# Splitting the last 384 columns of one 2 MB load into transfers of 119 and 9 rows, in a mixture of softmaxes on one core

## The chip, the core and the metric

The kernel runs on one core of a Trainium2 chip, the seven other cores idle. The metric is the device time of one execution in microseconds (us). Before the change it is 787.27 us, the median of three runs between 787.08 and 787.27 us.

## What is computed

There are 32 units (the batch). A unit has 128 rows, four heads and 4096 columns. In each row every head's 4096 logits go through a softmax; the four softmaxes are added, weighted by a softmax over the four numbers of `prior` in that row.

```python
def reference(logits, prior):            # (32, 128, 4, 4096), (32, 128, 4)
    prior_probs = softmax(prior)         # over the four heads
    softmax = np.exp(logits - logits.max(axis=-1, keepdims=True))
    softmax = softmax / softmax.sum(axis=-1, keepdims=True)
    return np.sum(prior_probs[..., None] * softmax, axis=2)   # (32, 128, 4096)
```

The input is 268.4 MB and the output 67.1 MB, all float32, and every byte moves once between HBM (the chip's main memory) and SBUF (the core's on-chip memory).

## The kernel before

The 128 rows of a unit are the 128 partitions of SBUF. The buffer `ring` has 12 slots; a slot holds one head of one unit, 128 x 4096 float32 (2 MB), so the ring holds three units. `place` (L106 of the kernel before) says which slot a head gets; `load` (L115, issuing at L120) brings heads that lie in neighbouring slots in one transfer of up to 8 MB.

A head goes through these steps: `peak` (VectorE, L128) takes the negated maximum of a row; `exp` (ScalarE, L133) exponentiates in place and sums; `recip` (VectorE, L139) inverts the sum. Heads 0 to 2 are then scaled and added up by TensorE: `diagonal` (GpSimd, L142) writes the scale on a diagonal matrix and `weigh` (L151) multiplies it with the exponentials into the accumulator `acc`. Head 3 is scaled by GpSimd (`scale`, L162) or directly by VectorE (L168). `evac` (ScalarE, L187) copies the accumulator out and `add_scaled` (GpSimd, L190) adds head 3 to it, in head 3's own slot; from that slot the unit is stored (L125).

The order of all this is written by hand: words such as `M3` (peak of head 3) or `L03+2` (load heads 0 to 2 of the unit after next) in the strings FIRST, STEADY and ORDER. All loads are issued by the sync engine's queue (SP). Stores of units 2 to 21 are issued by ScalarE's queue, the others by SP. At the start SP issues the four heads of unit 0 one by one (FIRST), then unit 1 in one transfer of 8 MB, then heads 0 to 2 of unit 2 (6 MB) and its head 3 (2 MB); ScalarE's queue issues the small load of `prior` beside the first. Later loads wait until their slots are free.

The transfers run on 16 DMA engines, which all queues share. A transfer of 128 rows is cut into 16 shares of 8 rows; each share reports its landing by itself, and whoever waits for the transfer waits for all 16 reports. The framework counts these reports on eight semaphores that the transfers take in turn; a transfer that takes one up again waits for the one that held it.

Of the kernel before, what the change touches and what calls it, by code (L numbers as in the profile page):

```python
# [63 lines left out]
    "R3@31 C3@31 T23@31 X112@31 T34@31 X212@31 A01@31 S23@31 A12@31 S34@31 S01@31 S12@31 "  # L64
]

BYPASS = {
    (27, 3), (28, 2), (28, 3), (29, 3), (30, 3), (31, 2), (31, 3),
}
# [3 lines left out]
def kernel(  # L73
# [6 lines left out]
    nc = tc.nc  # L80
    U, P, H, V = logits.shape
# [24 lines left out]
    def place(u, h):  # L106
        return (4 * u + h + (u == U - 1 and h == H - 1)) % SLOTS

    def slot(u, h, a=0, b=4):
        return ring[:, place(u, h), a * C : b * C]  # L110
# [2 lines left out]
        return slot(u, 3, a, b)  # L113

    def load(u, h=0, to=H):  # L115
        while h < to:
            s, n = place(u, h), 1
            while h + n < to and place(u, h + n) == s + n:
                n += 1
            nc.sync.dma_start(out=ring[:, s : s + n], in_=logits[u, :, h : h + n, :])  # L120
            h += n
# [26 lines left out]
    def weigh(u, h, a=0, b=4):  # L148
        e = slot(u, h)
        for k in range(a * C // W, b * C // W):  # L150
            nc.tensor.matmul(  # L151
                acc[:, k * W : (k + 1) * W], lhsT=diag[:, u % 2, h],
                rhs=e[:, k * W : (k + 1) * W],
                start=h == 0, stop=h == H - 2 or (u, k * W // C) in BYPASS and h == H - 3,
            )
# [33 lines left out]
    def add_scaled(u, a, b):  # L189
        nc.gpsimd.tensor_add(home(u, a, b), slot(u, 1, a, b), slot(u, 3, a, b))  # L190

    step = {
        "L": load, "S": store, "M": peak, "E": exp, "R": recip, "G": diagonal, "X": weigh,
        "C": weight, "Z": scale, "A": add_last, "B": add_head, "T": add_both, "V": evac,
        "P": add_scaled, "W": add_second,
# [11 lines left out]
    with tc.manual_schedule():  # L207
# [6 lines left out]
            out=ident, in_=ident, pattern=[[-1, P]], compare_op=ALU.is_equal, fill=0.0,  # L214
# [48 lines left out]
```

## Time and profile before

| | |
|---|---|
| median of three runs | 787.27 us |
| the profiled execution | 786.99 us |
| its span, first to last instruction | 785.2 us (so 1.75 us lie around it) |
| mean granted TensorE clock | 0.965 |
| moved | 335.90 MB, 428 GB/s over the span |
| busy: TensorE, VectorE, ScalarE, GpSimd | 679.0, 644.2, 548.0, 296.9 us |

The profile is one execution, taken by the hardware profiler. Beside the instructions the trace has each DMA packet (in this kernel, mostly one row of a transfer) with its start, length and size, though not the number of its DMA engine, and the moments at which the 16 shares of each transfer report. Where a time of a share or a packet is told below, it is read from these; times count from the first instruction.

### The profile page before, as it was taken

The numbers are of one execution on the slowest core, as the hardware profiler recorded it, in microseconds if no ns is written. First come the engines' busy times: TensorE is split into PE (matmuls) and PEld (weight loads), VectorE is DVE, ScalarE is ACT, GpSimd is POOL, SyncE is SP. The second block draws the span as 40 slices with busy tenths as digits, with TensorE's granted clock in tenths as the row PEclk, the third lists the DMA queues.
The fourth block names the chain that finished last, engine by engine and source line by source line (L and its number), as shares of the span: only waits on it lengthen the run. The fifth ranks groups of instructions, "written<-read, shape, count | busy, mean of one in ns | idle before, by whom it ended". The sixth has DMA issues, their size and how long they took to land.

```text
span 785.2 us, 4590 instructions
## 1 busy us (share of the span) xinstructions
PE 679.0 (86%) x1508; PEld 291.8 (37%) x1508; DVE 644.2 (82%) x326; ACT 548.0 (70%) x327; POOL 296.9 (38%) x244
## 2 busy tenths in 40 slices
PE   0959998888998989989889898998978998899996
PEld 0424444333443333434334333343333433334342
DVE  6489877897778977779877798777888877979895
ACT  2566876867668666687676776766857668779883
POOL 0053333433134332334323343323430544277892
PEclk9979999999999999989999999999989999999999
DMA  9999999999999999999999999999999999999998
GB/s 377 451 417 426 452 416 423 431 446 430 437 417 432 440 437 437 427 420 437 444 422 446 410 435 451 425 431 420 432 440 442 425 418 431 444 419 429 429 427 340
DMA packets 15336, 335.90 MB, mean 428 GB/s; under 512 B 1713, under 2 KB 1713, under 8 KB 2257
## 3 DMA queue, kind: packets, MB, share of 16 engines
q1 hardware_dynamic: 12384, 293.61, 87.1%
q10 hardware_dynamic: 2928, 42.01, 12.5%
q8 instruction: 12, 0.20, 0.1%
q14 instruction: 12, 0.09, 0.0%
HBM read 268.50 MB, written 67.11 MB: 427 GB/s over the span
## 4 chain that ended last, share of the span: by engine, by line
DMA 58%; DVE 12%; PE 10%; POOL 10%; issue 6%; ACT 3%; SPq 0%; POOLq 0%; ACTq 0%
DMA ring<-in_logits_dram 58%; DVE nmax L128 12%; PE acc L151 10%; POOL ring L190 7%; ACT ring L187 2%; ACT ring L133 1%; POOL ring L184 1%; POOL ring L162 1%; POOL diag L142 1%; DVE ring L168 0%; SPq L120 0%; DVE rden L139 0%; SPq L125 0%; POOLq L190 0%; POOLq L142 0%
## 5 line engine op out<-in xcount | busy, mean ns | idle before, releaser
L151 PE MATMUL acc<-ring,diag 128*128 128x512 f32 x1508 | 679.0, 611 | 99.3 <-ACT ring L187 63.7
L128 DVE TENSOR_REDUCE nmax<-ring 128x1 f32<-128x4096 f32 x128 | 563.1, 4409 | 115.9 <-DMA ring<-in_logits_dram 115.9
L133 ACT ACTIVATE ring<-ring,nmax 128x4096 f32<-128x4096 f32 x128 | 474.6, 3708 | 203.7 <-DVE nmax L128 203.3
L151 PEld LDWEIGHTS acc<-ring,diag 128*128 128x128 f32 x1508 | 291.8, 196 | 485.6 <-issue 356.3
L190 POOL TENSOR_TENSOR ring<-ring 128x1024 f32<-128x1024 f32 x69 | 162.3, 2371 | 19.6 <-ACT ring L187 12.9
L142 POOL TENSOR_SCALAR diag<-ident,rden,pp 128x128 f32<-128x128 f32 x96 | 42.9, 448 | 237.5 <-DVE rden L139 237.5
L158 POOL TENSOR_TENSOR wght<-rden,pp 128x1 f32<-128x1 f32 x33 | 6.2, 189 | 209.5 <-DVE rden L139 209.5
L187 ACT ACTIVATE ring<-acc 128x1024 f32<-128x1024 f32 x69 | 67.4, 1010 | 16.2 <-PE acc L151 12.0
L162 POOL TENSOR_SCALAR ring<-ring,rden,pp 128x2048 f32<-128x2048 f32 (+3 forms) x35 | 75.1, 2146 | 9.4 <-DVE rden L139 9.4
L168 DVE SCALAR_TENSOR_TENSOR ring<-ring,wght,acc 128x1024 f32<-128x1024 f32 x59 | 73.2, 1270 | 3.0 <-PE acc L151 1.3
L139 DVE RECIPROCAL rden<-dsum 128x1 f32<-128x1 f32 x128 | 19.3, 153 | 10.1 <-ACT ring L133 10.1
L133 ACT ACTIVATION_READ_ACCUMULATOR ring<-ring,nmax 128x1 f32 x128 | 24.2, 189 | 0.0
L184 POOL TENSOR_TENSOR ring<-ring 128x1024 f32<-128x1024 f32 x5 | 11.9, 2373 | 0.1
L218 DVE TENSOR_REDUCE pmax<-pr 32x128 f32<-32x512 f32 x1 | 0.7, 674 | 5.2 <-DMA pr<-in_prior_dram 5.2
L220 ACT ACTIVATE pr<-pr 32x512 f32<-32x512 f32 x1 | 0.6, 628 | 4.1 <-DVE pr L219 4.1
L168 DVE SCALAR_TENSOR_TENSOR ring<-ring,wght 128x1024 f32<-128x1024 f32 x2 | 2.5, 1283 | 0.3 <-POOL wght L158 0.3
L220 ACT ACT_TABLE_LOAD x1 | 1.3, 1283 | 1.2 <-PEq L247 1.2
L227 DVE STREAM_TRANSPOSE pp<-pn 32x128 f32<-32x128 f32 x4 | 1.2, 302 | 0.1
L221 DVE TENSOR_REDUCE pmax<-pr 32x128 f32<-32x512 f32 x1 | 0.7, 674 | 0.7 <-ACT pr L220 0.7
L223 DVE TENSOR_TENSOR pn<-pr,pmax 32x512 f32<-32x512 f32 x1 | 1.0, 1021 | 0.0
L222 DVE RECIPROCAL pmax<-pmax 32x128 f32<-32x128 f32 x1 | 0.9, 942 | 0.0
L219 DVE TENSOR_TENSOR pr<-pr,pmax 32x512 f32<-32x512 f32 x1 | 0.7, 680 | 0.0
(6 smaller groups left out, 0.9 us busy)
## 6 DMA issues: line engine op xcount, KB each, us to landing
ring<-in_logits_dram SPq DMA_DIRECT2D x27, 6144.0 KB, 34.3
ring<-in_logits_dram SPq DMA_DIRECT2D x43, 2048.0 KB, 25.9
out_dram<-ring ACTq DMA_DIRECT2D x20, 2048.0 KB, 16.0
out_dram<-ring SPq DMA_DIRECT2D x11, 2048.0 KB, 14.0
out_dram<-ring SPq DMA_DIRECT2D x4, 512.0 KB, 5.5
pr<-in_prior_dram ACTq DMA_DIRECT2D x1, 64.0 KB, 4.4
ring<-in_logits_dram SPq DMA_DIRECT2D x1, 39.4
```

The costliest lines, as they stand in the source:

```text
L128: nc.vector.tensor_reduce(out=nmax[:, u, h : h + 1], in_=slot(u, h), op=ALU.max, axis=AX.X, negate=True)
L133: nc.scalar.activation(slot(u, h), slot(u, h), AF.Exp, bias=nmax[:, u, h : h + 1], accum_out=dsum[:, u, h : h + 1],)
L139: nc.vector.reciprocal(rden[:, u, h : h + 1], dsum[:, u, h : h + 1])
L142: nc.gpsimd.tensor_scalar(out=diag[:, u % 2, h], in0=ident, scalar1=rden[:, u, h : h + 1], scalar2=pp[:, h, u : u + 1], op0=ALU.mult, op1= ...
L151: nc.tensor.matmul(acc[:, k * W : (k + 1) * W], lhsT=diag[:, u % 2, h], rhs=e[:, k * W : (k + 1) * W], start=h == 0, stop=h == H - 2 or (u ...
L158: nc.gpsimd.tensor_mul(wght[:, u, h : h + 1], rden[:, u, h : h + 1], pp[:, h, u : u + 1])
L162: nc.gpsimd.tensor_scalar(out=e, in0=e, scalar1=rden[:, u, h : h + 1], scalar2=pp[:, h, u : u + 1], op0=ALU.mult, op1=ALU.mult,)
L168: nc.vector.scalar_tensor_tensor(out=o, in0=slot(u, h, a, b), scalar=wght[:, u, h : h + 1], in1=more, op0=ALU.mult, op1=ALU.add,)
L184: nc.gpsimd.tensor_add(e, e, slot(u, 2, a, b))
L187: nc.scalar.activation(slot(u, 1, a, b), acc[:, a * C : b * C], AF.Copy)
L190: nc.gpsimd.tensor_add(home(u, a, b), slot(u, 1, a, b), slot(u, 3, a, b))
L220: nc.scalar.activation(pr, pr, AF.Exp)
```

## The change

Head 3 of unit 0 was one transfer of 128 rows x 4096 columns. It becomes three, one behind the other on SP's queue: 128 rows x 3712 columns, then the last 384 columns of rows 0 to 118, then those of rows 119 to 127. The same bytes move. A row of the two new transfers is 1,536 bytes. All other loads, and all steps of the order, stay as they are.

```diff
+EXTRA = 384
...
     def load(u, h=0, to=H):
+        if u == 0 and h == H - 1:
+
+            c = V - EXTRA
+            for p, q, i, j in ((0, P, 0, c), (0, 119, c, V), (119, P, c, V)):
+                nc.sync.dma_start(out=slot(u, h)[p:q, i:j], in_=logits[u, p:q, h, i:j])
+            return
         while h < to:
```

## The prediction

> **What bounds the kernel now.** I read the page's slices first, then the DMA queues, then the waits of the SP queue, and last the chain that ended last.
>
> ```profile
> DMA  9999999999999999999999999999999999999998
> GB/s 377 451 417 426 452 416 423 431 446 430 437 417 432 440 437 437 427 420 437 444 422 446 410 435 451 425 431 420 432 440 442 425 418 431 444 419 429 429 427 340
> ```
>
> ```profile
> q1 hardware_dynamic: 12384, 293.61, 87.1%
> q10 hardware_dynamic: 2928, 42.01, 12.5%
> q8 instruction: 12, 0.20, 0.1%
> q14 instruction: 12, 0.09, 0.0%
> HBM read 268.50 MB, written 67.11 MB: 427 GB/s over the span
> ```
>
> The reader is to see that the 16 DMA engines are busy in every slice (the shares of the queues add up to 99.7%), at 410 to 452 GB/s from the second slice to the last but one. No compute engine comes near: TensorE, the busiest, has 86%. The two small queues carry the program's own instructions.
>
> ```profile
> core 0: us, PE busy (x) PEld busy (x) DVE busy (x) ACT busy (x) POOL busy (x), PEclk, DMA share, GB/s
> ...
> 560.00:755.00 195.00, 176.17 (x393) 74.56 (x392) 165.94 (x82) 148.74 (x93) 96.88 (x71) 0.97 1.00 429
> 755.00:770.00 15.00, 14.61 (x34) 6.36 (x35) 14.42 (x7) 13.36 (x9) 14.69 (x11) 1.00 1.00 428
> 770.00:785.20 15.20, 8.24 (x20) 3.35 (x18) 7.68 (x7) 3.19 (x2) 0.71 (x3) 0.88 0.75 315
> ```
>
> The table of stretches says that the DMA share (the last column but one) falls below 1.00 only in the last 15 us. So some engines run out of work there, and the question is which one ends last.
>
> ```profile
> SPq L258 <- DMA out_dram<-ring: 4.2, 1, 4.2
> ```
>
> This wait of SP is the end of the kernel: the last store (512 KB, issued at 779.59 us) and nothing else. The chain of waits ends one step earlier:
>
> ```profile
> 767.68 10.58 PE acc L151 x24
> 778.26 0.02 issue
> 778.28 1.28 DVE ring L168
> ```
>
> The store's 16 shares report at 782.07 to 782.17 (eight), 782.21 to 783.10 (seven) and 784.17 (one). The first eight came 2.5 us after the issue: those engines were free. The last one is an engine with a backlog, 1.07 us behind the next. Its packets of 4,096 bytes start every 0.155 us without a gap up to 783.84. It is late since about 81 us: until 62 us the 16 reports of each transfer lie within 0.3 us, and from 81 us on the last is 1.3 us or more behind the median for most of the way (0.75 at the least, 2.7 near the end). Following its packets backwards, and those of the others, I find no engine dry before 769 us. **So the bound is one DMA engine's own work**: its bytes, and what it carried besides.
>
> **The change part by part.** Durations first. A row of 16,384 bytes starts 0.607 us after the one before it on the same engine, one of 4,096 bytes 0.155 us after. That is 0.0368 us per 1,000 bytes and 0.004 us per row. So 384 columns (1,536 bytes) less on a row save 0.0565 us, and a row of 1,536 bytes costs an estimated 0.061 us; the 2,048-byte rows of the `prior` load, 0.084 us long against 0.159 for 4,096, bear the slope out. A share's final mark takes 0.006 us.
>
> 1. The transfer of 128 rows gets shorter: 8 rows x 0.0565 = 0.452 us less on each of the 16 engines.
>
> 2. The 119 and 9 rows bring it back, but how they are shared the trace of before cannot show, for it has no such transfer. From below, an even spread: 8 rows x 0.061 and two marks = 0.50, so +0.05 us everywhere, nothing to speak of. From above, everything on one engine: 128 x 0.061 = 7.8 us, less 0.45. In between, what every transfer of before does: equal shares of whole rows (8 in those of 128 rows, 2 in that of 32). 119 is 7 x 17, so seven shares of 17; 9 makes nine shares of one. I take this, as nearest to the rows seen, and assume the small set of engines in the larger one. Then seven engines get 18 x 0.061 + 0.012 - 0.452 = **+0.66 us**, two get 0.061 + 0.006 - 0.452 = **-0.385 us**, and seven get **-0.45 us**. The sum over the engines hardly changes; the end depends on which group the late engine is in. Relieved are 9 of 16.
>
> The Trainium skill (DMA: Bandwidth & Descriptors, "Why a DMA increments its semaphore by 16 and not by 1") says that a transfer from the sync queue uses the largest number of engines up to 16 that divides its rows, and the lowest-numbered ones; by that the sum above holds as it stands, with engines 0 to 6 loaded. The same page ("Latency and other measured facts") calls engines 7 and 15 usually slower than the rest; by that the late engine is relieved by 0.385 or 0.45 us. The trace speaks against a slower engine as the cause: for the first 62 us all 16 land within 0.3 us. The lateness starts after an instruction packet of 16 KB (67.9 us, 1.1 us long), and it makes a jump, the last report going from 2.0 to 3.5 us behind the median, right after another (564.7 us).
>
> 3. Two more issues on SP: 2 x 0.42 us (the row `SPq L120` of the chain's start). They hide behind 6 MB already queued, which the engines need until 17.9 us; without that cover they cost 0.84 us.
>
> 4. Two new waits. With ten early transfers on eight semaphores, the 6 MB load of unit 2 now waits for the `prior` load (reported at 5.2 us) and its 2 MB load for head 0 of unit 0 (8.3 us), instead of being issued by 4.4 us. Behind them on SP stands the store of unit 0, issued at 58.75 us. The engines work on units 0 and 1 until 42.3 us, so this costs nothing, with 34 us to spare.
>
> 5. Head 3 of unit 0 lands up to 0.66 us later than 22.96 us, at 23.6. VectorE takes it up at 24.45, after head 2 (20.06 + 4.40). Hidden; 0.85 us is the margin.
>
> 6. Unit 1 lands up to 0.66 us after 42.31 us, which VectorE has waited for. Its work, and so the store of unit 0 (58.75 us) and the load behind it, come as much later. The queue then still holds work until 61.5 us, or 61.0 on a relieved engine; an engine starts on a fresh issue after about 0.85 us (779.59 to 780.44 at the end), and 58.75 + 0.66 + 0.85 = 60.3. Covered by 0.8 us; were it not, every us of dry queue would be a us of the end.
>
> 7. Every later pair of transfers that shares a semaphore is the same as before, moved by two places. I cost it at nothing; each waits for one eight transfers back, which had long landed.
>
> **The sum.** If the late engine is relieved by 0.45 us, the last report comes at 783.72 instead of 784.17. The next engine, at 783.10, comes to 783.76 at the worst, if it is a loaded one. The computing before it is no bar: engines without a backlog end at 782.2. So 786.99 - 0.45 to 0.41 = 786.5 for the profiled execution, which lay 0.28 us below the median; the median becomes 787.27 - 0.45 = **786.8 us**. About 0.2% (1.6 us) is what a measurement of this kernel can tell from no change, so this counts as no change.
>
> **The rivals.**
>
> *The late engine is among the seven loaded ones.* It ends 0.66 us later: 787.9 us. For it: 7 of 16, and the trace does not number the engines. Against it: nothing but the count. Also within 0.2%.
>
> *The split does nothing.* The 128 rows end up evenly spread: +0.05 us, 787.3 us. Against it: 119 rows cannot be equal shares on 16 engines.
>
> *A fixed price per transfer (slower).* If the engines had to end one transfer before they start the next, each of the two added ones would cost its latency. From the last store, on engines without a backlog: 2.6 us from issue to report (779.59 to 782.19), of which moving 8 rows takes 1.24, so 1.4 us each, 2.8 us for two: 790.1 us. It decides when a transfer does not overlap the one queued behind it. Against it: the queued 2 MB transfers of unit 0 report 4.89 us apart, and their rows alone take 8 x 0.607 = 4.86. The same side has all 128 rows on one engine: 7.8 - 0.45 = 7.3 us, 794.6 us if it is the late engine; on one of the least delayed, which report 4.0 us before the late one for a transfer near the end (760.72 against 764.68), 7.3 - 4.0 = 3.3 us, 790.6 us. The Trainium skill (the same page, "Rules for kernel authors") speaks for this side, as it asks for 128 partitions and at least 1 MiB per transfer and calls those under 64 KB mostly overhead. By its formula of 2.0 us per transfer (given for another issuing path) two would cost 4 us; the 4.89 us spacing disagrees for queued transfers.
>
> *A gain over 0.2%.* The late engine's extra work is at most the 2 us that separate it from the free ones, and the change takes away 0.45 of it. Only a different assignment of the instruction packets could do more.
>
> **How the numbers follow.** Relieved 0.47 and loaded 0.36 (9 to 7); no effect 0.08; a price per transfer or a lump on one engine 0.06; a gain over 0.2% 0.03. So faster by over 0.2%: 0.03, within: 0.91, slower: 0.06. The range must reach the two likeliest and the no-effect case (0.91 together), with 0.2 to 0.5 us for the scatter of medians: 786.3 to 788.1 us.
>
> **What would show it.** In the changed trace the 119-row transfer should show seven shares with 17 rows of 1,536 bytes and the 9-row one nine with one. Before any instruction packet, unit 1's 16 reports should fall into groups about 1.1 us apart, where before they lay within 0.3 us. The last store's latest report should move by -0.45 (right) or +0.66 us (the first rival). A load that starts on a dry queue near 61 us would show point 6 wrong, a gap between the three transfers' packets the price per transfer. The prediction is wrong if the end moves by more than 1.6 us.

## The result and the profile after

The changed kernel takes 788.46 us, the median of 22 runs (788.12 to 788.88); the kernel before, in 22 runs beside it, 786.96 us (786.75 to 788.09). The ratio is 1.0016, with a 95% interval of 1.0010 to 1.0022: slower by some 1.3 us by this ratio (the medians lie 1.5 us apart), clear of the interval though below the 0.2% that the prediction took for the limit of what can be told. It went the other way than forecast and lies 0.36 us above the stated range. The profiled execution took 788.36 us with a span of 786.6 us, against 786.99 and 785.2.

Two rows of the page first. The columns of the rate are 40 equal slices; the share of the DMA engines is 9 tenths or more as before.

```profile
GB/s 381 422 426 437 398 428 422 437 442 441 424 420 431 440 435 438 419 429 442 431 441 416 429 432 446 434 426 424 434 445 423 442 414 431 448 414 430 429 429 350
```

Against before, the second slice (20 to 39 us) falls from 451 to 422 GB/s and the fifth (79 to 98 us) from 452 to 398. The transfers are busy all the time and move less: each packet takes longer.

The queues of the page of the changed kernel (packets, time, share of 16 engines' span) have 144 packets more, which are the 128 short rows and 16 marks, and no queue that is new:

```profile
q1 hardware_dynamic: 12528, 293.61, 87.2%
q10 hardware_dynamic: 2928, 42.01, 12.5%
```

Its end, in the waits of SP and in the chain of waits:

```profile
SPq L266 <- DMA out_dram<-ring: 4.2, 2, 3.0
```

```profile
769.13 10.58 PE acc L159 x24
779.71 0.02 issue
779.73 1.28 DVE ring L176
```

The last store is still what SP waits for, 4.2 us in all, and the same last pieces, of the same length, stand 1.45 us later than before. So the last steps were not changed, they were delayed.

The same in the stretches, the last column the rate. A stretch seems to count whole packets, so only equal stretches compare. First the kernel before, then the changed one:

```profile
core 0: us, PE busy (x) PEld busy (x) DVE busy (x) ACT busy (x) POOL busy (x), PEclk, DMA share, GB/s
18.00:44.00 26.00, 22.34 (x48) 9.68 (x48) 12.59 (x7) 12.99 (x8) 1.34 (x3) 1.00 1.05 451
...
82.00:110.00 28.00, 28.00 (x67) 12.45 (x66) 23.97 (x13) 23.45 (x14) 8.71 (x8) 1.00 1.00 428
```

```profile
core 0: us, PE busy (x) PEld busy (x) DVE busy (x) ACT busy (x) POOL busy (x), PEclk, DMA share, GB/s
18.00:44.00 26.00, 22.54 (x48) 9.69 (x48) 11.25 (x7) 12.96 (x8) 1.35 (x3) 1.00 1.04 435
...
82.00:110.00 28.00, 28.00 (x67) 12.45 (x66) 24.39 (x12) 23.61 (x13) 9.16 (x9) 1.00 1.00 413
```

What VectorE and then SP make of it (start, duration, instruction; in the bracket the idle time before), first in the kernel before, then in the changed one:

```profile
42.33 4.42 DVE L128 TENSOR_REDUCE nmax<-ring 128x1 f32<-128x4096 f32 x1 [13.41 <-DMA ring<-in_logits_dram]
...
58.75 0.35 SPq L125 DMA_DIRECT2D out_dram<-ring  x1
```

```profile
43.74 4.42 DVE L136 TENSOR_REDUCE nmax<-ring 128x1 f32<-128x4096 f32 x1 [14.57 <-DMA ring<-in_logits_dram]
```

```profile
2.15 1.60 SPq L122 DMA_DIRECT2D ring<-in_logits_dram  x3
3.79 4.79 SPq L128 DMA_DIRECT2D ring<-in_logits_dram  x3
60.18 0.35 SPq L133 DMA_DIRECT2D out_dram<-ring  x1
```

VectorE gets unit 1 at 43.74 us (42.33 before), and the store of unit 0 is issued at 60.18 us (58.75 before). Both are 1.4 us late, and so is the end: the last store's latest report comes at 785.61 us instead of 784.17.

The reports and packets of the three new transfers show why. The shortened transfer reports at 22.25 to 22.59 us, 0.37 to 0.47 us earlier, as costed. The 119-row transfer has seven reports and the 9-row one nine. The Trainium skill (DMA: Bandwidth & Descriptors, "Why a DMA increments its semaphore by 16 and not by 1") gives these counts, and the trace agrees with 7 and 9. But the seven engines need until 24.16 to 24.37 us, some 1.85 us for 17 rows: their first rows start 0.061 us apart, as estimated, and from 22.2 us on the rows take 0.09 to 0.13 us each. At the same time the 64 KB rows of unit 1 that other engines have begun take 3.2 us instead of 2.42. Unit 1's reports fall into two groups, nine at 42.36 to 42.60 us and seven at 43.60 to 43.72, where before all 16 came at 42.06 to 42.31. **Nobody was relieved: nine engines are 0.3 us later and seven 1.4 us.**

Summed over the engines, the packets of 20 to 40 us take 0.83 us more per engine than in before, those of 60 to 110 us another 1.2 us; after that the packets of the two kernels take the same.

### The profile page after: what moved, and what is told of

Read it like the earlier page. It is cut to its first block, busy times and chain, and to the rows that moved or that the text cites. A ratio compares the mean times of both kernels' runs of the same rounds, so it can differ in the third digit from the quotient of the medians.

```text
span 786.6 us, 4595 instructions
## 1 busy us (share of the span) xinstructions
PE 680.7 (87%) x1508; PEld 292.4 (37%) x1508; DVE 644.3 (82%) x326; ACT 548.2 (70%) x327; POOL 297.0 (38%) x244
## 4 chain that ended last, share of the span: by engine, by line
DMA 58%; DVE 12%; POOL 10%; PE 10%; issue 5%; ACT 4%; SPq 0%; POOLq 0%; ACTq 0%
DMA ring<-in_logits_dram 58%; DVE nmax L136 12%; PE acc L159 10%; POOL ring L198 7%; ACT ring L141 3%; ACT ring L195 2%; POOL ring L192 1%; POOL ring L170 1%; POOL diag L150 1%; DVE ring L176 0%; SPq L122 0%; SPq L128 0%; DVE rden L147 0%; SPq L133 0%; POOLq L198 0%
```

## The experiments

The theory now is **destination**: an engine is slowed where it fills SBUF partitions that share their way in with partitions another engine is filling at that moment. By this theory each engine has a way of its own in a transfer of 128 rows, and in transfers of 119, 9 or other numbers of rows it has not. Rivals: **uneven shares** (seven engines simply have more to do), **short rows** (rows of 1,536 bytes are slow for everybody), **source** (their HBM addresses get in each other's way), and a price per transfer. The diffs of e1 to e4, e8, e10 and e11 are against the changed kernel, those of e5, e6, e7 and e9 against the kernel before; where only lines with + stand, the rest of the edit is left out, such as the condition `if u == 0 and h == H - 1:`. Each time is compared with runs of before on the same chip.

### Shape and share, taken apart

```diff
# e1_small_even
-            for p, q, i, j in ((0, P, 0, c), (0, 119, c, V), (119, P, c, V)):
+            for p, q, i, j in ((0, P, 0, c), (0, 112, c, V), (112, P, c, V)):
# e2_whole_uneven
+            for p, q, i, j in ((0, 112, 0, V), (112, 119, 0, V), (119, P, 0, V)):
# e3_whole_even
+            for p, q, i, j in ((0, 96, 0, V), (96, 112, 0, V), (112, P, 0, V)):
```

> The 384 columns again in 1,536-byte rows behind the rest, but as transfers of 112 and 16 rows, so that all 16 engines get the same 8 small rows (7 and 1). Small-row theory (short rows slow the engines whoever carries them; in the changed kernel the packets of 20 to 40 us lost 0.83 us on the mean engine): a similar loss of 0.5 to 1 us at 20 to 40 us and an end 0.5 to 1.5 us later than before. Uneven-share theory (the seven engines with 18 rows set the end): nothing lost beyond 0.05 us, the end as before within 0.2 us.

Measured: 787.12 us against 787.18, ratio 1.000 (0.9991 to 1.0009). Unit 1 lands 0.42 us late on all engines alike. In the stretch from 18 to 44 us the rate is nearly that of before:

```profile
18.00:44.00 26.00, 23.05 (x48) 9.98 (x48) 12.26 (x7) 13.10 (x8) 1.34 (x3) 1.00 1.05 448
```

As many short rows, evenly shared, cost half as much on the mean engine as in the changed kernel and nothing at the end. Short rows as such are not it. The uneven-share theory had the end right, but not the 0.42 us.

> Head 3 of unit 0 in whole rows of 16,384 bytes, as transfers of 112, 7 and 9 rows: seven engines get 9 rows, two get 8, seven get 7, so 0.61 us more and less without any short row. Small-row theory: no loss in the rate at 20 to 40 us (432 GB/s kept); the end moves only by whether the late engine is among the seven, at most 0.6 us either way. Uneven-share theory: the end comes 0.6 us later, and in proportion to the changed kernel's 1.4 us up to 0.9 us.

Measured: 793.44 us against 787.18, ratio 1.0078 (1.0065 to 1.0090), 6.3 us slower. Neither theory of the time had this; whole rows lost far more than short ones.

> Three transfers of whole rows, 96, 16 and 16: eight rows on every engine, so nothing of the change is left but two more transfers with their issues and the two new waits of the sync queue. Both theories: as before within 0.2 us. If two more transfers cost a fixed time, 1 us or more later.

Measured: 793.02 us against 787.18, ratio 1.0074 (1.0061 to 1.0086), 5.8 us slower, with every engine carrying the same 8 rows as before. So a loss needs no uneven shares either. A 16-row transfer of one row per engine, 0.607 us of work, takes 1.5 to 2.1 us from the reports of the one ahead of it to its own. The stretch shows how hard it hits:

```profile
18.00:44.00 26.00, 23.02 (x48) 9.95 (x48) 11.17 (x6) 13.13 (x8) 1.34 (x3) 1.00 1.05 352
```

The DMA share is 1.05, as in before, and the rate 352 instead of 451 GB/s: busy engines, slow packets. What is left is what the rows lie on at the two ends, or a price of 2.9 us for each added transfer.

### Another place

```diff
# e4_unit8
-        if u == 0 and h == H - 1:
+        if u == 8 and h == H - 1:
```

> The same split of 384 columns into 119 and 9 rows, but for head 3 of unit 8, in the steady part, where the engines no longer run in step. Small-row theory: a loss of about 0.8 us on the mean engine where that load runs (about 225 us) and an end 0.5 to 1.5 us later. If the loss needs the engines in step, or the delay of the first store, as at the start: the end within 0.7 us of before, by the shares alone.

Measured: 788.11 us against 787.18, ratio 1.0011 (1.0002 to 1.0020), 0.9 us slower. In the profiled execution the packets of 200 to 220 us take 1.2 us more per engine. The loss does not need the start, nor engines in step.

### Destination or source

```diff
# e5_halves
+            for p, q in ((0, 64), (64, P)):
+                nc.sync.dma_start(out=slot(u, h)[p:q], in_=logits[u, p:q, h])
# e6_even_near
+            near = logits[u].rearrange("p h v -> (p h) v")
+            for p, q in ((0, 96), (96, 112), (112, P)):
+                nc.sync.dma_start(out=slot(u, h)[p:q], in_=near[p:q])
# e7_one_pitch48
+            far = logits[u].rearrange("p h v -> (p h) v")
+            nc.sync.dma_start(out=slot(u, h), in_=far[0 : 3 * P : 3])
# e8_after_near: the transfers of 119 and 9 rows read from one closed block
+            near = logits[u].rearrange("p h v -> (p h v)")
...
+                block = near[p * EXTRA : q * EXTRA].rearrange("(p v) -> p v", v=EXTRA)
+                nc.sync.dma_start(out=slot(u, h)[p:q, c:V], in_=block)
```

> Head 3 of unit 0 as two transfers of whole rows, 0 to 63 and 64 to 127: every engine gets 4 and 4 rows, as in before. Destination theory (an engine is slow where the SBUF partitions it fills are also being filled by other engines on the same way in; a page gives 16 such ways, of which 64 neighbouring partitions reach only 8): each half moves at half the rate, head 3 lands 4.9 us later and the end comes 4 to 6 us later. Source theory (the rows' addresses in HBM get in each other's way): the spacing of the engines' rows is halved against before, no reason for a loss of that size. Number-of-transfers theory (a price for each transfer, read from three even transfers costing 5.8 us, or 2.9 each): 2.9 us later.

Measured: 792.30 us against 787.10, ratio 1.0064 (1.0051 to 1.0078), 5.2 us slower. Two transfers lose nearly as much as three, so it is not a price per transfer. The first half reports at 23.00 to 23.56 us, some 5 us after the load ahead of it, and the second 4.9 us later, where 4 rows per engine are 2.43 us of work: each half runs at half the rate. Most of its rows take 1.1 to 1.28 us, against 0.61 in before.

```profile
18.00:44.00 26.00, 22.25 (x48) 9.59 (x48) 10.98 (x6) 12.95 (x8) 1.34 (x3) 1.00 1.01 352
```

The Trainium skill (SBUF — State Buffer, "Door 1: The DMA port swizzle (why `[64,N]` ≈ `[32,N]`)") says that the 128 partitions are reached through 16 ports, four neighbouring partitions and the four 32 further on through the same one, and that partitions 0 to 63 reach eight of them. By that a half runs at half the rate; the trace agrees, with 4.9 us for 2.43. For 16 neighbouring rows, on four ports, it would be a fourth; the trace has 1.5 to 2.1 us for 0.607, three to four tenths, with neighbouring transfers overlapping.

> The three even transfers of 96, 16 and 16 whole rows again, to the same partitions, but read from one closed block of 2 MB of unit 0's logits (rows 16 KB apart) instead of every fourth row (64 KB apart); head 3 of unit 0 is so filled with other logits. Destination theory: still 5.8 us later than before. Source theory: the loss is gone, within 0.5 us of before.

Measured: 792.91 us against 787.10, ratio 1.0074 (1.0059 to 1.0090): 5.8 us, to the tenth what the same partitions cost with the other addresses.

> Head 3 of unit 0 as one transfer of 128 rows, as in before, but read from rows 48 KB apart instead of 64 KB, so that engines start 384 KB apart as in the 96-row transfer; head 3 of unit 0 is so filled with other logits. Destination theory: as before, within 0.3 us. Source theory: a loss of some us, as with the 96 rows.

Measured: 787.09 us against 787.10, ratio 1.000 (0.9991 to 1.0009). Other addresses, the usual partitions: no loss.

```profile
18.00:44.00 26.00, 22.51 (x48) 9.68 (x48) 12.58 (x7) 12.88 (x8) 1.36 (x3) 1.00 1.04 449
```

> The changed kernel, with the 119 and 9 short rows read from one closed block of HBM (rows 1,536 bytes apart) instead of rows 64 KB apart; the last 384 columns of head 3 of unit 0 are so filled with other logits. Destination theory: the same loss as the changed kernel, 0.8 us on the mean engine at 20 to 40 us and an end 1.3 us later than before. Source theory: the loss is mostly gone, the end within 0.7 us of before.

Measured: 788.38 us against 787.10, ratio 1.0018 (1.0009 to 1.0027), 1.3 us slower, as the changed kernel. Unit 1's reports fall into the same groups, 42.30 to 42.57 and 43.43 to 43.76 us.

```profile
18.00:44.00 26.00, 22.96 (x48) 9.83 (x48) 11.16 (x7) 12.90 (x8) 1.36 (x3) 1.00 1.04 433
```

With e6, e7 and e8 the source is out: three other patterns of addresses, in the changed split, the even one and the whole transfer, left the time where the partitions had put it. Destination stands, as the theory that is left and by its forecast for the halves (4.9 us at head 3, 4 to 6 us at the end; 4.9 and 5.2 came). No run keeps a transfer's rows per engine and its source and changes its partitions alone.

### Which engine is late, and the size

```diff
# e9_probe_before (against before), e10_probe_after (against the changed kernel)
+        if 6 <= u <= 20 and h == H - 1:
+            n = u - 5
+            nc.sync.dma_start(out=mark[0:n, n - 1], in_=logits[u, 0:n, 0, 0:64])
# e11_768
-EXTRA = 384
+EXTRA = 768
```

> The kernel before with 15 tiny loads added (1 row of 256 bytes behind unit 6's head 3, 2 rows behind unit 7's, up to 15 behind unit 20's), whose data nobody uses. A transfer of n rows uses n engines, the first n, so the reports of the tiny loads number the engines by their lateness. If the late engine is one of the seven that carried the 17 short rows, a report as late as the last one of its neighbours appears among the tiny loads of at most 7 rows; if not, only among those of 8 and more. The end: within 0.5 us of before.

Measured: 787.03 us in one run against 787.26. The tiny loads have as many reports as rows. With 5 rows the last comes 0.3 us after the one ahead of it (254.34 us, 254.04); with 6 rows it comes 2.4 us after (281.01, 278.57), and a late one stays in all the larger loads up to 11 rows, at 1.4 us or more. So from 281 to 401 us the late engine is the sixth, **one of the seven** that got 17 short rows. From 12 rows on a second engine, the twelfth, is as late (packets of the tiny load at 425.41 and 425.52 us), and after 500 us no tiny load tells the engines apart. That the sixth is also the one that ends last is likely, for the end of the changed kernel came 1.44 us later, as the seven did at 42 us, but it is not shown.

> The changed kernel with the same 15 tiny loads. If the end of the changed kernel is set by the engine that was late before, the late report appears at the same number of rows in both; if another engine has taken its place, at another number.

Measured: 788.54 us in one run against 787.26 of the kernel before. Again the late report appears with 6 rows (282.44 us, the next 280.89). The same engine is last in the middle of the run; at the end of the changed kernel five engines report within 0.1 us (785.52 to 785.61).

> The changed kernel with 768 columns split off instead of 384. Destination theory, with the late engine among the seven: rows of 3,072 bytes that fill partitions other engines fill too take twice as long, so the 0.83 us on the mean engine and the 1.4 us on the seven at 40 us double to about 1.7 and 2.8 us, and the end comes 2.4 to 3 us later than before. Costing the seven by bytes alone, 10 rows more of 3,072 bytes: 1.2 us.

Measured: 790.95 us against 787.26, ratio 1.0046 (1.0033 to 1.0060), 3.7 us slower: three times what bytes alone would cost and more than the doubling forecast. At 42 us the seven are 3.3 us late (2.8 expected) and the mean engine 2.0.

## Why the prediction was wrong, point by point

- **The bound held.** The engines stay busy and the last report of the last store ends the kernel, before and after. Its latest share moved by 1.44 us and the span by 1.4; where one engine ended 1.07 us after all others, five now end within 0.1 us.
- **Point 1 held**: 0.37 to 0.47 us less for the shortened transfer, 0.452 forecast.
- **The way of sharing in point 2 held**: seven shares of 17 and nine of one, and with them the 1.1 us forecast between the two groups of unit 1's reports (42.60 and 43.72 us for the last of each). The even spread and the lump on one engine are out.
- **The price of a row in point 2 failed.** 0.061 us was worked out from rows of the transfers of before, in which, by the destination theory, no engine is in another's way. Seventeen rows took 1.85 us instead of 1.04, and they slowed others' rows: the seven engines came out at +1.4 us instead of +0.66, the nine at +0.3 instead of -0.385 or -0.45. "The sum over the engines hardly changes" was the wrong sentence: it rose by 0.83 us per engine. Against the forecast by shares both groups are late by about the same 0.7 us: the slower rows cost every engine alike, on top of the uneven shares, and 0.66 + 0.7 makes the 1.4 us of the seven. With no engine relieved, the forecast of 786.8 us had no way to come true, whichever group the late engine was in.
- **The likelier guess about the late engine failed too**, as far as the tiny loads reach: from 281 to 401 us it is the sixth, among the loaded. The rival that had it there had the right sign and less than half of the size, 0.66 us for 1.4.
- What the Trainium skill (DMA: Bandwidth & Descriptors, "Latency and other measured facts") says of engines 7 and 15, that they are usually slower, does not fit here: the sixth was late, and before 62 us none was.
- **Points 3, 4 and 7 are not what cost the time**: the experiment with 112 and 16 short rows has the same number of transfers and of new waits, and ends with before.
- **Points 5 and 6**: head 3 landed at 24.55 us, 0.1 us after VectorE could have taken it. The delay of unit 1 was 1.4 us instead of 0.66, more than the 0.8 us of cover for the store behind it; the nine less delayed engines ended the work ahead of it at 61.8 to 62.0 us, and a fresh issue of 60.18 us starts at about 61.0, so the queue just held.
- **The fixed price per transfer is out as a mechanism.** Its 2.8 us for two transfers is not in the experiment with 112 and 16 rows. What the even splits of whole rows lost, 5 to 6 us, is bigger and follows the partitions.

What stays open: the lateness at 42 us and that of the end agree in the changed kernel (1.4 and 1.44 us), but not everywhere. With evenly shared short rows 0.42 us early became -0.1 at the end, and with 768 columns 3.3 became 4.0. Between 67 and 110 us, where the late engine falls behind, its delay differed by up to half a microsecond from kernel to kernel. The versions that are uneven in unit 0 also lose some 0.8 us per engine between 80 and 100 us (0.55 in the run with tiny loads), the even ones next to nothing; the uneven split in unit 8 loses nothing more after its own stretch. That the two groups of engines then collide in the same way would fit, but no run tested it.

## What to carry to other kernels

In these runs the 128-row transfers took the time of their rows, and transfers cut by rows, even into equal shares, took longer; the theory that stands is that a row keeps its time only as long as no other engine is filling partitions through the same way in. Before a duration is taken from a row of the profile for a transfer of another shape, ask what kept that row fast: here, by that theory, it was the pattern of the destination, which no row of before could show. And where moving work from one engine to others is costed as a sum of zero, check the total of the packets' times and not only the shares.

## What the runs showed of the hardware

- With two transfers of 64 neighbouring rows in place of one of 128 the kernel takes 5.2 us more (792.30 against 787.10 us), though the engines carry the same rows. The Trainium skill (DMA: Bandwidth & Descriptors, "Rules for kernel authors") advises against two halves because both use the same engines and follow one another; the loss here is beyond that, for each half ran at half the rate.
- Rows 16, 48 or 64 KB apart in HBM made no difference that the runs could tell (792.91 against 793.02 us for the even split, each with its own runs of before near 787.1; 787.09 against 787.10 for the whole).
- A tiny load of n rows gives n reports. A late one comes with 6 rows and stays with 7 to 11, 24.25 us apart as the loads are, which fits the same first n engines each time. Added behind the loads, such transfers number the engines at no cost in time that one run could show (787.03 us).
